# Queries and keys of a neighbourhood attention stored as 128 whole rows, with bias tables and modulation stepped at other rates

## The chip, the cores and the metric

The kernel runs on one core of a Trainium2 chip. The metric is device time of one execution in microseconds, median over several runs. The engines are named as in the profile: PE (matmuls), PEld (weight loads of PE), DVE, ACT and POOL (elementwise work), SP (issues DMAs only). ACT and POOL issue DMAs too; a DMA stands in the instruction order of the engine that issues it.

## The reference

Two blocks stand one behind the other: a two-layer block (below) and a one-layer block with dilated attention. The change is in the first one, in both of its layers. A layer projects 2048 latent and 256 context tokens (1024 wide) with one matrix and splits the result; three mixers work on the parts, among them the neighbourhood attention:

```python
hx = rmsnorm(x, norm_w[l]) * (1.0 + scale_x[:, None, :]) + shift_x[:, None, :]
(fx, fgx, nqx, nkx, nvx, ngx, gqx, gkx, gvx, ggx, zfx, zbx) = jnp.split(hx @ w_in[l], IN_SPLITS, axis=-1)
...
na_x = neighbourhood_attention(split_heads(nqx, NA_HEADS), split_heads(nkx, NA_HEADS),
                               split_heads(nvx, NA_HEADS), nkc_h, nvc_h, rpb[l])
...
# inside: 6 heads of 64, an 8 x 16 neighbourhood on a grid 64 wide, a bias from rpb, and all context keys
s_loc = jnp.einsum('brqhd,brikhd->bhrqik', qg, kg).astype(jnp.float32) + bias[None]
s_ctx = jnp.einsum('brqhd,bchd->bhrqc', qg, kc).astype(jnp.float32)
p = jax.nn.softmax(jnp.concatenate([s_loc, s_ctx], axis=-1), axis=-1)
...
x_new = x + gate_x[:, None, :] * (mix_x @ w_out[l])
```

`shift`, `scale` and `gate` (the modulation) are products of a small vector with w_ada.

## The kernel before

All matmuls on large matrices are done on a split of both operands into a hi and a lo part: three products (`MM3`) stand for one.

**The input projection** (`b1_inproj`, class `InProj`) runs once per layer as 13 blocks of output columns. `InProj.block` goes through the groups of a block (tokens); each group is 24 matmuls (8 pieces of the inner dimension, 3 products) into one PSUM tile `mm` (a pool of 5), which an `evac` function empties. Block 4 is the Fourier input (18 groups of 128 tokens in layer 0, 16 in layer 1), blocks 5 to 7 are the keys (`nk`, 128 columns each), 8 to 10 the queries (`nq`), 11 and 12 gates (`fg`). Blocks 5 to 12 have groups of 512 tokens: four and one of 256 in layer 0; in layer 1 the queries and gates have only the four.

While a block runs, the weights of the next are made: `prep` loads 6 and then 2 pieces into one buffer `wraw` (SP, line 244), ACT writes `whi` (line 252), POOL writes `wlo` (line 253).

**Evacuation of queries and keys** (`qk_evac`): ACT writes the scaled hi part (`evh`, lines 465 and 468), DVE the lo part (`evl`, lines 466 and 469), both into tiles of one pool of four (`ev`). POOL then stores them to DRAM (line 455, names `kl`, `ql`): hi and lo for keys, hi, lo and hi again for queries. The scratch is `[6 heads, 3 or 2 copies, 64, TT]`, so that a store of 128 partitions is written as 2 heads of 64 rows. The two `fg` blocks store `ev` tiles to `gT` from POOL too (line 446), as 128 rows of one step.

**Extra work** is a generator, `ip.extra`, advanced `ip.rate` times after each group: `tables` makes the attention's bias tables for both layers (`Bias.make`, 17 steps a layer: POOL loads `rpt`, stores `rp`, loads 12 pieces `bt` (line 1070), DVE works on `bt` (lines 1075, 1079 and 1080), POOL stores `be` and `bi` (line 1083)); `ada` makes a part of the modulation (`Ada.part`: loads of `adaw`, 512 KB each, into two buffers on SP (line 105), 8 steps of matmuls `adaps` (line 120), a row and its store). `more` says which generator runs in blocks 4 to 6 (first) and in blocks 7 to 12 (second), each of the two with its own SBUF pool `ipa`, which takes the same memory one after the other. What is left of a generator at the end of its blocks runs there.

**The attention** (`na`) loads per group of 512 queries two tiles `Q` (hi over lo, and lo over hi; `load_q`, line 1102), and per head a tile `Ks` of keys (hi over lo; `load_k`, line 1108), one group ahead. The first of them go through POOL, all later ones through SP. Three pairs of heads times five groups are 15 query groups in layer 0, and 12 in layer 1. The attention runs beside the linear attention and other work (the mixers).

The tile framework decides the order of instructions on each engine from the order of the code and from its own estimates, and sets the waits: for operands, for the release of a buffer or of memory that a later pool takes over, and for one of eight DMA semaphores used in turn by each issuing queue.

Of the kernel before, what the change touches and what calls it, by code (L numbers as in the profile page):

```python
# [23 lines left out]
TT = T + TC  # L24
# [3 lines left out]
def f(ap):  # L28
    return ap.bitcast(F32)


def dap(ap, off, dims):
    return bass.AP(tensor=ap.tensor, offset=ap.offset + off, ap=[list(d) for d in dims])
# [34 lines left out]
def dtile(K, shape, name):  # L68
    return K.dram.tile(list(shape), F32, name=name)
# [95 lines left out]
class InProj:  # L165
# [4 lines left out]
    def __init__(s, K, w, tiles, CMAX, wp, xp, ev):  # L170
        s.K, s.w, s.tiles, s.CMAX, s.wp, s.xp, s.ev = K, w, tiles, CMAX, wp, xp, ev
        s.xt = {}
        s.late = []
        s.extra = None
        s.rate = 1
        s.hd = None
        s.XB = 3

# [95 lines left out]
    def block(s, b):  # L274
        nc = s.K.nc
        kind, segs, groups, evac, prod = s.blocks[b]
        if prod:
            s.scale(0)
            s.scale(1)
            s.produce(0)  # L280
            s.scale(2)
            s.produce(1)
        C = sum(n for _, n in segs)
        todo = b + 1 < len(s.blocks)
        s.W[b + 1] = []
        ng = len(groups)
        w = s.W[b]
        for i, g in enumerate(groups):
            if prod:
                s.produce(i + 2)  # L290
                s.scale(i + 3)
            ps = s.mm.tile([128, 512], F32, name="mm", tag="mm")

            order = [(k, x, y) for k in range(8) for x, y in MM3]
            if prod:
                order.sort(key=lambda o: (o[1], o[0]))
            for n, (k, x, y) in enumerate(order):
                st, sp = n == 0, n == 23
                if kind == "t":
                    nc.tensor.matmul(ps[:, :C], s.hT[x][:, k, 128 * g:128 * g + 128], w[k][y][:, :C], start=st, stop=sp)  # L300
                else:
                    t0, tn = g
                    nc.tensor.matmul(ps[:C, :tn], w[k][y][:, :C], s.hT[x][:, k, t0:t0 + tn], start=st, stop=sp)  # L303
            new = evac(ps, g, i) or iter(())
            next(new, None)
            s.step()
            s.late.append(new)
            if s.extra is not None:
                for _ in range(s.rate):
                    next(s.extra, None)  # L310
            want = (8 * (i + 1) + ng - 1) // ng
            while todo and len(s.W[b + 1]) < want:
                s.W[b + 1] += s.prep(s.blocks[b + 1][1], len(s.W[b + 1]))
        del s.W[b]
# [10 lines left out]
def b1_inproj(K, A, l, xsrc, mod, S, keep, more=None):  # L325


    nc, tc = K.nc, K.tc
# [3 lines left out]
    full = l == 0  # L332
# [6 lines left out]
    with ExitStack() as es:  # L339
# [108 lines left out]

        def qk_evac(nm, r0, scale):


            ns = 3 if nm == "q" else 2

            def out(x, y, t0, tn):
                nc.gpsimd.dma_start(dap(S[nm], ((r0 // 64) * ns + x) * 64 * TT + t0, [[64 * ns * TT, 2], [TT, 64], [1, tn]]), f(y[:, :tn]))

            def go(ps, g, i):
                t0, tn = g
                hi = ev.tile([128, 512], F32R, name="evh", tag="ev")
                lo = ev.tile([128, 512], F32R, name="evl", tag="ev")  # L460
                if nm == "q" and tn == 512:
                    for h in range(2):
                        src = dap_sb(ps, 32 * h + 479, [[-64, 8], [-1, 32]])
                        oh, ol = (x[:, 256 * h:256 * h + 256].rearrange("p (a b) -> p a b", b=32) for x in (hi, lo))
                        nc.scalar.activation(out=oh, in_=src, func=AF.Copy, scale=scale)
                        nc.vector.scalar_tensor_tensor(out=ol, in0=src, scalar=scale, in1=f(oh), op0=ALU.mult, op1=ALU.subtract)
                else:
                    nc.scalar.activation(out=hi[:, :tn], in_=ps[:, :tn], func=AF.Copy, scale=scale)
                    nc.vector.scalar_tensor_tensor(out=lo[:, :tn], in0=ps[:, :tn], scalar=scale, in1=f(hi[:, :tn]), op0=ALU.mult, op1=ALU.subtract)
                for x, y in ((0, hi), (1, lo), (2, hi))[:ns]:  # L470
                    out(x, y, t0, tn)
            return go

        tx = list(range(16))
# [47 lines left out]
            ip.end()  # L522
        for bs, fill in ((range(4, 7), 0), (range(7, run), 1)):
            with tc.tile_pool(name="ipa", bufs=1, side="right", reuse_waits="tile") as p:
                ip.rate = 1
                ip.raw = lambda: p.tile([128, 768], F32, name="wraw", tag="wraw", bufs=1)
                if more[fill] is not None:
                    ip.extra = more[fill](p, lambda: mm.tile([128, 512], F32, name="adaps", tag="mm"), lambda: pt.tile([128, 256], F32, name="adat", tag="pt"))
                for b in bs:
                    ip.block(b)  # L530
                for _ in ip.extra or ():
                    pass
                ip.end()
# [57 lines left out]
def b1_scratch(K, l):  # L591
    s = {}
    n = f"l{l}"
    s["vh"] = dtile(K, [2, 32, 40, 384], "vh" + n)
    s["vc"] = dtile(K, [256, 384], "vc" + n)
    s["f"] = dtile(K, [TT, 256], "f" + n)
    s["g"] = dtile(K, [TT, 768], "g" + n)
    s["gq"], s["gk"], s["gv"] = (s["g"][:, a:b] for a, b in ((0, 192), (192, 384), (384, 768)))
    s["la"] = dtile(K, [2, TT, 192], "la" + n)
    s["gT"] = dtile(K, [1024, TT], "gT" + n)  # L600
    s["h"] = dtile(K, [18 if l == 0 else 16, 128, 1024], "h" + n)
    s["q"] = dtile(K, [6, 3, 64, TT], "q" + n)
    s["k"] = dtile(K, [6, 2, 64, TT], "k" + n)
    s["mixT"] = dtile(K, [1024, TT], "mixT" + n)
    return s

# [480 lines left out]
def na(K, A, l, S, B, p, pp, nps):  # L1087

    nc = K.nc
    full = l == 0  # L1090
    groups = [(pr, g) for pr in range(3) for g in range(5 if full else 4)]

    q0 = [nc.gpsimd]
    rd = dtile(K, [3, 5, 1024], f"rd{l}")

    def load_q(pr, g):

        n = 512 if g < 4 else TC
        out = []
        for x in range(2):  # L1100
            q = p.tile([128, 2, 512], F32R, name="Q", tag="Q", bufs=4)
            q0[0].dma_start(f(q[:, :, :n]), dap(S["q"], (2 * pr * 3 + x) * 64 * TT + 512 * g, [[TT, 128], [192 * TT, 2], [1, n]]))
            out.append(q)
        return out

    def load_k(pr, hh):
        k = p.tile([128, TT], F32R, name="Ks", tag="Ks", bufs=3)
        q0[0].dma_start(f(k[:]), dap(S["k"], (2 * pr + hh) * 128 * TT, [[TT, 128], [1, TT]]))
        return k

    def load_vc(pr):
# [1166 lines left out]
def program(nc, tc, A, out):  # L2278
    K = Ctx()
    with ExitStack() as es:  # L2280
# [21 lines left out]
                    yield from part  # L2302
            return go

        more = ((tables, ada((0, 2))), (None, ada((1, 2))))

        S = [b1_scratch(K, l) for l in range(2)]
        S2 = b2_scratch(K)
        keeps = [ExitStack() for l in range(2)]
# [69 lines left out]
```

## Time and profile before

| | |
|---|---|
| median of 3 runs | 4462.8 us (4462.49 to 4475.38) |
| profiled execution | 4484.28 us, its span 4482.5 us |
| PE busy | 4165.0 us (93%) |
| DVE, ACT, POOL busy | 1757.1, 1646.8, 1526.9 us (39, 37, 34%) |
| mean granted clock of PE | 0.949 |
| DMA | 637.13 MB, 610668 packets, mean 142 GB/s |

The granted clock is a share of TensorE's full speed; 1.0 and 0.5 are its two levels. The profile is of one execution that took 21.5 us more than the median of the runs. PE is the engine that is nearest to always busy, so what counts is where it stands idle and where its clock is granted at half.

### The profile page before, as it was taken

The page shows a single profiled execution, that of the slowest core. Times are in us where ns is not written, and L with a number is a line of the kernel's source. Part 1 is how long each engine was busy: PE and PEld are TensorE (multiplying, and loading weights), DVE is VectorE, ACT ScalarE, POOL GpSimd, SP SyncE. Part 2 cuts the span into 40 slices and gives each one's busy share as a digit, 9 for nine tenths or more (in the row PEclk, how much of TensorE's full clock was granted, in tenths as well). Part 3 has the DMA queues.
Part 4 walks back from the last instruction along what each step waited for, and adds up shares of the span by engine and source line. Part 5 has one row for each costly group of instructions (what it writes and reads, how often), then busy time and mean ns, then how long its engine had stood idle before and what let it go on. Part 6 is the DMA issues. An engine that isn't in the chain of part 4 may idle for free.

```text
span 4482.5 us, 79595 instructions
## 1 busy us (share of the span) xinstructions
PE 4165.0 (93%) x29633; PEld 3517.6 (78%) x29633; DVE 1757.1 (39%) x4996; ACT 1646.8 (37%) x4121; POOL 1526.9 (34%) x1944
## 2 busy tenths in 40 slices
PE   7999679989999999987898998999999999998998
PEld 6988469867767799865896777889998877776886
DVE  5331003366752362200235674553640025665222
ACT  5141114355661151511435656242222215664221
POOL 4234333212422332233321241444742340553333
PEclk8999889999999999998998999999999998888999
DMA  6435435466566544245546666542331156745221
GB/s 201 144 106 123 120 96 192 152 179 184 180 214 203 170 139 144 87 100 112 189 159 179 179 194 193 176 142 81 103 109 50 62 172 158 173 127 147 91 94 61
DMA packets 610668, 637.13 MB, mean 142 GB/s; under 512 B 188632, under 2 KB 487964, under 8 KB 606826
## 3 DMA queue, kind: packets, MB, share of 16 engines
q1 hardware_dynamic: 499546, 477.70, 36.3%
q0 software_dynamic: 99184, 136.27, 10.6%
q10 hardware_dynamic: 11552, 18.08, 1.1%
q8 instruction: 235, 3.85, 0.4%
q14 instruction: 151, 1.24, 0.1%
HBM read 424.26 MB, written 207.09 MB: 141 GB/s over the span
## 4 chain that ended last, share of the span: by engine, by line
PE 38%; issue 4%; DMA 3%; POOL 3%; DVE 2%; ACT 1%; SPq 1%; POOLq 0%; DVEq 0%; ACTq 0%
PE mm L300 7%; PE mm L303 5%; PE ops L1420 4%; PE tps L2173 3%; PE tps L2232 3%; PE gps L580 2%; PE apo L1827 2%; PE apt L1807 2%; PE aps L1786 2%; PE aps L1789 2%; POOL wlo L253 1%; PE po L1224 1%; PE go L991 1%; PE pl L1199 1%; PE gc L918 1%
## 5 line engine op out<-in xcount | busy, mean ns | idle before, releaser
L300 PE MATMUL mm<-whi,hTh 128*128 128x304 f32 (+2 forms) x1424 | 422.0, 300 | 2.1 <-ACT hTh L220 2.1
L300 PE MATMUL mm<-wlo,hTh 128*128 128x304 f32 (+2 forms) x1424 | 419.7, 298 | 0.0
L253 POOL TENSOR_TENSOR wlo<-wraw,whi 128x128 fp32r<-128x128 f32 (+3 forms) x384 | 224.1, 612 | 485.7 <-ACT whi L252 475.9
L300 PE MATMUL mm<-whi,hTl 128*128 128x304 f32 (+2 forms) x1424 | 380.9, 296 | 0.0
L303 PE MATMUL mm<-hTh,whi 128*128 128x512 f32 x600 | 239.9, 400 | 64.7 <-ACT whi L252 30.5
L300 PE MATMUL mm<-whi,h2h 128*128 128x256 f32 x1024 | 293.0, 290 | 2.4 <-ACT h2h L220 2.4
L300 PE MATMUL mm<-wlo,h2h 128*128 128x256 f32 x1024 | 285.7, 283 | 0.0
L300 PEld LDWEIGHTS mm<-whi,hTh 128*128 128x128 f32 x1424 | 270.6, 190 | 2.9 <-ACT hTh L220 2.8
L300 PE MATMUL mm<-whi,h2l 128*128 128x256 f32 x1024 | 272.1, 284 | 0.0
L300 PEld LDWEIGHTS mm<-wlo,hTh 128*128 128x128 f32 x1424 | 270.5, 190 | 0.0
L300 PEld LDWEIGHTS mm<-whi,hTl 128*128 128x128 f32 x1424 | 256.9, 189 | 1.1 <-issue 1.1
L252 ACT ACTIVATE whi<-wraw 128x128 fp32r<-128x128 f32 (+3 forms) x416 | 122.9, 356 | 339.5 <-DMA wraw<-in_w_in 322.2
L303 PE MATMUL mm<-hTh,wlo 128*128 128x512 f32 x600 | 236.6, 394 | 8.4 <-POOL wlo L253 8.4
L580 PE MATMUL gps<-gh,whi 128*128 128x256 f32 x816 | 233.8, 287 | 6.2 <-ACT gh L155 6.2
L303 PE MATMUL mm<-hTl,whi 128*128 128x512 f32 x600 | 234.7, 391 | 0.0
L580 PE MATMUL gps<-gh,wlo 128*128 128x256 f32 x816 | 232.9, 286 | 0.0
L580 PE MATMUL gps<-gl,whi 128*128 128x256 f32 x816 | 232.3, 285 | 0.0
L1420 PE MATMUL ops<-owh,omh 128*128 128x512 f32 x544 | 214.0, 393 | 0.0
L1420 PE MATMUL ops<-owh,om 128*128 128x512 f32 x544 | 211.9, 390 | 0.1
L1420 PE MATMUL ops<-owl,omh 128*128 128x512 f32 x544 | 211.7, 389 | 0.0
L303 PEld LDWEIGHTS mm<-hTh,whi 128*128 128x128 f32 x600 | 119.4, 199 | 99.8 <-ACT whi L252 31.2
L300 PEld LDWEIGHTS mm<-whi,h2h 128*128 128x128 f32 x1024 | 194.8, 190 | 2.7 <-ACT h2h L220 2.7
(482 smaller groups left out, 11041.1 us busy)
## 6 DMA issues: line engine op xcount, KB each, us to landing
qkv<-gl SPq DMA_DIRECT2D x72, 384.0 KB
adaw<-in_w_ada SPq DMA_DIRECT2D x48, 512.0 KB
Q<-ql SPq DMA_DIRECT2D x44, 512.0 KB
hl<-evk SPq DMA_DIRECT2D x68, 256.0 KB
gl<-hl SPq DMA_DIRECT2D x17, 1024.0 KB
om<-mixTl SPq DMA_DIRECT2D x34, 512.0 KB
gTl<-ev POOLq DMA_DIRECT2D x67, 256.0 KB, 3.9
wraw<-in_w_in SPq DMA_DIRECT2D x32, 512.0 KB
```

The lines of the kernel that those rows point to most:

```text
L252: nc.scalar.activation(out=hi[:, :C], in_=raw[:, k], func=AF.Copy)
L253: (eng or nc.gpsimd).tensor_tensor(out=lo[:, :C], in0=raw[:, k], in1=f(hi[:, :C]), op=ALU.subtract)
L300: nc.tensor.matmul(ps[:, :C], s.hT[x][:, k, 128 * g:128 * g + 128], w[k][y][:, :C], start=st, stop=sp)
L303: nc.tensor.matmul(ps[:C, :tn], w[k][y][:, :C], s.hT[x][:, k, t0:t0 + tn], start=st, stop=sp)
L580: nc.tensor.matmul(ps.rearrange("p (t n) -> p t n", t=2), W[b][k][y][:, 128 * j:128 * j + 128], h[x][:, :, k], start=n == 0, stop=n == 23)
L1420: nc.tensor.matmul(ps, m[x][:, k], W[k][y][:, 512 * n:512 * n + 512], start=k == j == 0, stop=k == 7 and j == 2)
L1786: nc.tensor.matmul(ps[:, hh, cs], q[:, qs], k[:, ks], start=True, stop=False, skip_group_check=True)
L1789: nc.tensor.matmul(ps[:, hh, cs], q[h, qs], kl[h, ks], start=False, stop=True, skip_group_check=True)
L1807: nc.tensor.transpose(pt[:, hh, c], ec[:, hh, 128 * c:128 * c + 128], K.ident)
L1827: nc.tensor.matmul(o[rr], V[:, r * (16 // DIL[br]) + b - full + c * full, rr], et[:, hh, c], start=not full or c == 0, stop=not full or c ...
L2173: nc.tensor.matmul(ps, m[u][:, k], b.Wo[k][v][:, 512 * n:512 * n + 512], start=k == b.KS[0] and j == 0, stop=k == b.KS[7] and j == 2)
L2232: nc.tensor.matmul(ps, X[x][:, k], b.Wg[k][y][:, ns], start=j == 0, stop=j == 23)
```

## The change

Stores: the scratch of queries and of keys becomes `[3 pairs of heads, 2, 128, TT]`, a store's destination 128 rows of one step, and the third store of the queries (hi again) goes. Loads: each `Q` and each `Ks` is loaded by two DMAs of 64 partitions. Extra work: in layer 0 the tables take 2 steps a group, `ada` 1 step every second group; in layer 1 `ada` moves from blocks 7 to 12 into blocks 4 to 6, also 1 step every second group.

```diff
--- before.py
+++ after.py
@@ -173,6 +173,7 @@
         s.late = []
         s.extra = None
         s.rate = 1
+        s.due = 0
         s.hd = None
         s.XB = 3
 
@@ -306,7 +307,9 @@
             s.step()
             s.late.append(new)
             if s.extra is not None:
-                for _ in range(s.rate):
+                s.due += s.rate
+                while s.due >= 1:
+                    s.due -= 1
                     next(s.extra, None)
             want = (8 * (i + 1) + ng - 1) // ng
             while todo and len(s.W[b + 1]) < want:
@@ -448,12 +451,6 @@
 
         def qk_evac(nm, r0, scale):
 
-
-            ns = 3 if nm == "q" else 2
-
-            def out(x, y, t0, tn):
-                nc.gpsimd.dma_start(dap(S[nm], ((r0 // 64) * ns + x) * 64 * TT + t0, [[64 * ns * TT, 2], [TT, 64], [1, tn]]), f(y[:, :tn]))
-
             def go(ps, g, i):
                 t0, tn = g
                 hi = ev.tile([128, 512], F32R, name="evh", tag="ev")
@@ -467,8 +464,8 @@
                 else:
                     nc.scalar.activation(out=hi[:, :tn], in_=ps[:, :tn], func=AF.Copy, scale=scale)
                     nc.vector.scalar_tensor_tensor(out=lo[:, :tn], in0=ps[:, :tn], scalar=scale, in1=f(hi[:, :tn]), op0=ALU.mult, op1=ALU.subtract)
-                for x, y in ((0, hi), (1, lo), (2, hi))[:ns]:
-                    out(x, y, t0, tn)
+                for x, y in enumerate((hi, lo)):
+                    nc.gpsimd.dma_start(S[nm][r0 // 128, x, :, t0:t0 + tn], f(y[:, :tn]))
             return go
 
         tx = list(range(16))
@@ -522,7 +519,8 @@
             ip.end()
         for bs, fill in ((range(4, 7), 0), (range(7, run), 1)):
             with tc.tile_pool(name="ipa", bufs=1, side="right", reuse_waits="tile") as p:
-                ip.rate = 1
+
+                ip.rate = 2 if full and not fill else 0.5
                 ip.raw = lambda: p.tile([128, 768], F32, name="wraw", tag="wraw", bufs=1)
                 if more[fill] is not None:
                     ip.extra = more[fill](p, lambda: mm.tile([128, 512], F32, name="adaps", tag="mm"), lambda: pt.tile([128, 256], F32, name="adat", tag="pt"))
@@ -599,8 +597,9 @@
     s["la"] = dtile(K, [2, TT, 192], "la" + n)
     s["gT"] = dtile(K, [1024, TT], "gT" + n)
     s["h"] = dtile(K, [18 if l == 0 else 16, 128, 1024], "h" + n)
-    s["q"] = dtile(K, [6, 3, 64, TT], "q" + n)
-    s["k"] = dtile(K, [6, 2, 64, TT], "k" + n)
+
+    s["q"] = dtile(K, [3, 2, 128, TT], "q" + n)
+    s["k"] = dtile(K, [3, 2, 128, TT], "k" + n)
     s["mixT"] = dtile(K, [1024, TT], "mixT" + n)
     return s
 
@@ -1099,13 +1098,15 @@
         out = []
         for x in range(2):
             q = p.tile([128, 2, 512], F32R, name="Q", tag="Q", bufs=4)
-            q0[0].dma_start(f(q[:, :, :n]), dap(S["q"], (2 * pr * 3 + x) * 64 * TT + 512 * g, [[TT, 128], [192 * TT, 2], [1, n]]))
+            for y in range(2):
+                q0[0].dma_start(f(q[64 * y:64 * y + 64, :, :n]), S["q"][pr, x ^ y].rearrange("(h r) t -> r h t", h=2)[:, :, 512 * g:512 * g + n])
             out.append(q)
         return out
 
     def load_k(pr, hh):
         k = p.tile([128, TT], F32R, name="Ks", tag="Ks", bufs=3)
-        q0[0].dma_start(f(k[:]), dap(S["k"], (2 * pr + hh) * 128 * TT, [[TT, 128], [1, TT]]))
+        for x in range(2):
+            q0[0].dma_start(f(k[64 * x:64 * x + 64]), S["k"][pr, x, 64 * hh:64 * hh + 64])
         return k
 
     def load_vc(pr):
@@ -2302,7 +2303,7 @@
                     yield from part
             return go
 
-        more = ((tables, ada((0, 2))), (None, ada((1, 2))))
+        more = ((tables, ada((0, 2))), (ada((1, 2)), None))
 
         S = [b1_scratch(K, l) for l in range(2)]
         S2 = b2_scratch(K)
```

In POOL's queue in layer 0, at the first key block (`kl` are stores of keys; `bt`, `be`, `bi` belong to the bias tables; `wlo` are weights of a later block), stood before:

```order
L1083 DMA bi_82<-bt 32x2x1200 x3
L455 DMA kl_93<-evh 2x64x512
L455 DMA kl_93<-evl 2x64x512
L455 DMA kl_93<-evh 2x64x512
L455 DMA kl_93<-evl 2x64x512
L1070 DMA bt<-rp_4320 32x15x40 x2
L455 DMA kl_93<-evh 2x64x512
L455 DMA kl_93<-evl 2x64x512
L1070 DMA bt<-rp_4320 32x15x40 x2
L455 DMA kl_93<-evh 2x64x512
L455 DMA kl_93<-evl 2x64x512
L1070 DMA bt<-rp_4320 32x15x40 x2
```

and now stands:

```order
L1082 DMA bi_82<-bt 32x2x1200 x3
L468 DMA kl_93<-evh 128x512
L468 DMA kl_93<-evl 128x512
L468 DMA kl_93<-evh 128x512
L1069 DMA bt<-rp_4058 32x15x40 x12
L468 DMA kl_93<-evl 128x512
L468 DMA kl_93<-evh 128x512
L468 DMA kl_93<-evl 128x512
L468 DMA kl_93<-evh 128x512
L254 TENSOR_TENSOR wlo<-wraw,whi 128x128 x2
L1082 DMA be_83<-bt 32x2x1200 x3
L468 DMA kl_93<-evl 128x512
```

The twelve loads of the second table's `bt`, two behind each pair of stores before, now stand in one row behind the third store, and the stores of `be` follow within the same block.

In SP's queue in layer 0, from the weights of block 7 on (`wraw` are weights of the projection in pieces of 6 and 2, `adaw` weights of the modulation, `adagb` its bias), stood before:

```order
L244 DMA wraw<-in_w_in 128x6x128
L244 DMA wraw<-in_w_in 128x2x128
L105 DMA adaw<-in_w_ada 128x1024 x2
L244 DMA wraw<-in_w_in 128x6x128
L144 DMA adagb<-in_b_ada 2x256 x4
L244 DMA wraw<-in_w_in 128x2x128
L244 DMA wraw<-in_w_in 128x6x128
L105 DMA adaw<-in_w_ada 128x1024
L244 DMA wraw<-in_w_in 128x2x128
L105 DMA adaw<-in_w_ada 128x1024
L244 DMA wraw<-in_w_in 128x6x128
L105 DMA adaw<-in_w_ada 128x1024 x3
```

and now stands:

```order
L245 DMA wraw<-in_w_in 128x6x128
L245 DMA wraw<-in_w_in 128x2x128
L245 DMA wraw<-in_w_in 128x6x128
L105 DMA adaw<-in_w_ada 128x1024 x2
L144 DMA adagb<-in_b_ada 2x256 x4
L245 DMA wraw<-in_w_in 128x2x128
L245 DMA wraw<-in_w_in 128x6x128
L245 DMA wraw<-in_w_in 128x2x128
L245 DMA wraw<-in_w_in 128x6x128
L245 DMA wraw<-in_w_in 128x2x128
L245 DMA wraw<-in_w_in 128x6x128
L105 DMA adaw<-in_w_ada 128x1024 x2
```

The pair of `adaw` loads stands behind the six-piece load of the next block's weights instead of ahead of it, and the later `adaw` loads stand further back, with whole blocks of weights between them.

In POOL's queue in layer 0, where the attention starts (`ke`, `ss` and `oacc` belong to the linear attention), stood before:

```order
L1108 DMA Ks<-kl_93 128x2304
L1102 DMA Q<-ql_92 128x2x512 x2
L1108 DMA Ks<-kl_93 128x2304
L935 TENSOR_TENSOR ke<-qkv,e_8366 128x192
L1141 DMA vl<-vhl_85 110x4x128
L59 TENSOR_SCALAR ss<-ss 128x4
L1126 DMA bias<-bi_82 32x880
L60 TENSOR_TENSOR ss<-ss,mhalf 128x4
```

and now stands:

```order
L1109 DMA Ks<-kl_93 64x2304 x2
L934 TENSOR_TENSOR ke<-qkv,e_8351 128x192
L1102 DMA Q<-ql_92 64x2x512 x3
L59 TENSOR_SCALAR ss<-ss 128x4
L1102 DMA Q<-ql_92 64x2x512
L934 TENSOR_TENSOR ke<-qkv,e_8456 128x192
L60 TENSOR_TENSOR ss<-ss,mhalf 128x4
L1109 DMA Ks<-kl_93 64x2304
L1015 TENSOR_TENSOR oacc<-oacc,ss 128x384
L59 TENSOR_SCALAR ss<-ss 128x4
L1109 DMA Ks<-kl_93 64x2304
```

The three loads that the first scores need (keys of one head, two `Q` tiles) have become six, and the last of them and the second head's keys stand behind more of the linear attention's work.

## Rows read from the trace of the kernel before

**Rows 1.** Busy time by stretch: us, PE, PEld, DVE, ACT, POOL, clock, DMA share, GB/s
```profile
397.17:422.40 25.23, 25.23 (x122) 20.77 (x121) 2.50 (x4) 3.97 (x11) 15.36 (x25) 1.00 0.45 109
371.98:669.68 297.70, 224.23 (x1026) 178.19 (x1024) 26.88 (x52) 37.35 (x111) 107.55 (x169) 0.87 0.46 110
1898.07:1920.42 22.35, 22.35 (x98) 18.01 (x97) 2.50 (x4) 2.31 (x5) 6.46 (x10) 1.00 0.33 77
1898.07:2151.17 253.10, 205.46 (x906) 160.48 (x904) 20.88 (x43) 34.75 (x106) 85.38 (x136) 0.90 0.45 105
```

**Rows 2.** The same of line 120's matmuls alone, first stretch
```profile
371.90:669.70 297.80, 6.00 (x64) 1.35 (x64) 0.87 0.46 110
```

**Rows 3.** Waits of PE, 372 to 670: total, times, longest (us)
```profile
PE mm L303 <- ACT whi L252: 24.1, 1, 24.1
PE adaps L120 <- DMA adaw<-in_w_ada: 20.0, 3, 13.8
PE mm L303 <- DVE evl L469: 8.5, 1, 8.5
PE mm L303 <- POOL wlo L253: 8.4, 1, 8.4
PE mm L303 <- DVE evl L466: 6.9, 3, 6.0
PE mm L303 <- ACT ev L445: 5.6, 1, 5.6
```

**Rows 4.** Waits of PE, 1898 to 2151
```profile
PE adaps L120 <- DMA adaw<-in_w_ada: 28.0, 2, 15.1
PE mm L303 <- DVE evl L469: 7.0, 2, 6.3
PE mm L303 <- ACT whi L252: 6.4, 1, 6.4
PE mm L303 <- DVE evl L466: 6.2, 1, 6.2
```

**Rows 5.** DMA issues, 372 to 670: count, KB each, median us to landing
```profile
ql<-evh POOLq DMA_DIRECT2D x24, 256.0 KB, 13.6
...
kl<-evh POOLq DMA_DIRECT2D x12, 256.0 KB, 11.0
...
bt<-rp POOLq DMA_DIRECT2D x12, 75.0 KB, 11.4
```

**Rows 6.** DMA issues, 340 to 352, the first bias table
```profile
bt<-rp POOLq DMA_DIRECT2D x12, 75.0 KB, 3.4
```

**Rows 7.** The first two key stores, 378 to 380, by tile
```profile
DMA to landing us min/median/max: 9.3/10.2/11.0
```

**Rows 8.** The gate stores, 640 to 669, by tile
```profile
DMA to landing us min/median/max: 2.3/3.9/4.5
```

**Rows 9.** Waits of ACT, 372 to 670
```profile
ACT evh L468 <- DMA kl<-evh: 50.4, 10, 8.6
```

**Rows 10.** Timeline of SP, 430 to 500: start, duration, line
```profile
435.78 31.96 SPq L105 DMA_DIRECT2D adaw<-in_w_ada  x2
467.79 2.80 SPq L244 DMA_DIRECT2D wraw<-in_w_in  x1
```

**Rows 11.** Waits of SP, 372 to 670
```profile
SPq L105 <- DMA bi<-bt: 15.4, 1, 15.4
```

**Rows 12.** Timeline of POOL, 300 to 386
```profile
342.13 7.89 POOL L1070 DMA_DIRECT2D bt<-rp  x12
```

**Rows 13.** Busy time in the two mixer stretches, columns as in Rows 1
```profile
760.00:1560.00 800.00, 758.11 (x6708) 606.17 (x6707) 389.98 (x1206) 358.77 (x875) 231.17 (x267) 0.98 0.60 184
2260.00:2950.00 690.00, 647.92 (x5830) 522.23 (x5829) 390.25 (x1126) 340.95 (x813) 208.73 (x257) 0.96 0.60 181
```

**Rows 14.** Waits of PE, 2260 to 2950
```profile
PE sc L1158 <- DMA Q<-ql: 1.5, 1, 1.5
```

**Rows 15.** Timeline of SP, 950 to 975
```profile
956.22 0.38 SPq L1102 DMA_DIRECT2D Q<-ql  x1
```

## The prediction

> **What bounds the kernel now.** I read the busy times first: PE is at 93%, so the question is where it stands still or is granted half its clock. The windows view then gives the two stretches in which the changed stores run, the projection blocks 5 to 12 of each layer [rows 1]. An undisturbed block of five groups takes 25.23 us, one of four 22.35 us, both at clock 1.00, with PE busy all the time. Layer 0 has eight blocks of five, 201.8 us, and 6.0 us of modulation matmuls [rows 2]: 207.8 us of work. The stretch takes 297.7 us, with PE busy for 224.2 and clock 0.87. Layer 1 has three blocks of five and five of four, 187.4 us, with the 6.0 us 193.4; its stretch takes 253.1 us, at 0.90. The surplus is 89.9 + 59.7 = 149.6 us. Of it PE is idle for 73.5 + 47.6 = 121.1 us; the other 28.5 us are work that ran longer, at a mean clock of 0.87 and 0.90 instead of 1.00.
>
> The waits of PE name what ended each idle time, and their sums are the same 73.5 and 47.6 us [rows 3, 4]. They fall into three classes:
> - **Evacuation.** DVE's evl, ACT's ev and, in layer 0, POOL's wlo: 8.5 + 6.9 + 5.6 + 8.4 = 29.4 us; in layer 1 evl and whi: 7.0 + 6.2 + 6.4 = 19.6 us. Behind all stands the landing of the stores: an ev buffer comes free when its store has landed, 11.0 us (keys) or 13.6 us (queries) after POOL issued it [rows 5], and ACT waited 50.4 us for key stores to land [rows 9]. What stands behind a waiting evacuation on ACT (whi) or behind a waiting store on POOL (wlo) is late with it.
> - **SP held by the tables.** 24.1 us, once, in layer 0. SP stood for 31.96 us at two adaw loads and only then issued the next wraw load, at 467.79 [rows 10]; the last thing waited for was bi<-bt [rows 11], since the second pool's adaw takes over the memory of the tables.
> - **Modulation.** adaps waited for adaw: 20.0 + 28.0 us.
>
> **The change part by part.**
>
> Store shape. The gate stores of the same size, already written as 128 rows of one step, land after 2.3 to 4.5 us, median 3.9 [rows 8]. The first two key stores, which follow no other key store, needed 9.3 and 11.0 us [rows 7]. So it is not the pile of stores alone, and I take 3.9 us for all new stores; the bounds are 2.3 and 11.0. What it is worth: two evacuations fit into the four ev buffers, and PE makes a group in 25.23 / 4.5 = 5.6 us (the last is a half one), so a pair may be held for 11.2 us before PE is paced by it. At 11.0 to 13.6 us plus making and issuing it is over that; at 3.9 us it is far under it, and five PSUM tiles (28 us of PE) cover a late one. The evacuation class goes, 49.0 us. The third query store goes as well; it occupied only POOL and the queue, so it counts nothing by itself once the others land fast.
>
> [...]
>
> Tables at two steps a group. The work is the same; the second table's twelve bt loads stand in a row on POOL, which took 7.89 us for the first table [rows 12]. Behind them wait a key store and later wlo. The cover is the 28 us of PSUM; without it the cost would be about 8 us. Those loads landed in 3.4 us without key stores around them and in 11.4 us among them [rows 5, 6], so bi lands earlier, within blocks 5 and 6, and SP's wraw load for block 8 stands ahead of adaw anyway. The 24.1 us go; should the tables still be late, they hold adaw, which is first needed some groups later.
>
> Modulation at one step in two groups. Steps lie 11.2 us apart instead of 5.6, with the same two buffers, so each load has twice the time; in layer 1 it starts in block 4. adaw and wraw still share SP's queue in order, and an adaw that waits for its buffer holds back the wraw behind it. Between nothing left and all 48.0 us left with their share of slow clock, 48.0 / 121.1 x 28.5 = 11.3, so 0 to 59 us, I take 15, nearer to the lower end, since the slow stores that held ACT's whi, POOL's wlo and with them SP's wraw are gone.
>
> Slow clock. Undisturbed blocks stand at 1.00 and the stretches with stops at 0.87 and 0.90 [rows 1], so I let the 28.5 us go with the stops; what stays is in the 15.
>
> Loads in halves. 27 query groups times two tiles and 12 heads are 66 loads, of which SP issues 58; so there are 58 more on SP, 0.38 us each [rows 15], 22 us, and 8 on POOL at some 0.66 (7.89 / 12), 5 us. They lie in stretches in which PE is idle for 41.9 of 800 and 42.1 of 690 us [rows 13]. PE waited 1.5 us for a Q in one of them [rows 14], as a group is loaded one group ahead. The cover is that lead; the worst is 27 us. The scheduler also orders the mixers anew, which could gain or lose: below nothing I allow 10 us, a quarter of one stretch's idle time. I take +4 us, nearest to the row, for the later first scores.
>
> [...]
>
> **The sum.** 149.6 - 15 - 4 = 130.6 us less. The profiled execution took 4484.3 us and would take 4353.7. It lies 21.5 us above the median of the runs; I put that down to this execution and take the same difference from the median: 4462.8 - 130.6 = 4332.2 us.
>
> **The rivals.**
> - **SP's queue takes over** (the weights wait in place of the evacuation). For it: wraw is one buffer, adaw still stands between its loads, with three adaw in one row at the end. Against it: within an undisturbed block the weights came in time. Price: the modulation waits stay, 48.0, and whi's 6.4, with their clock share, 12.8: 67.2 in place of the 15. Gain 149.6 - 67.2 - 4 = 78.4, 4384 us.
> - **The stores stay slow** (their landing is traffic, not shape). For it: bt loads too went from 3.4 to 11.4 us in that company, and the gate stores were measured in a later part of the stretch. Against it: the first key stores. Then evacuation stays, 49.0 with 11.5 of clock: gain 130.6 - 60.5 = 70.1, 4393 us.
> - **The halves come late** (slower). Place: the first score of each of the 27 query groups, behind four Q loads on SP instead of two, among the linear attention's loads. It decides from 130.6 / 27 = 4.8 us a group on; at 6 us, 162 us are lost and the time is 4494 us. For it: SP issues in order. Against it: [rows 14].
> [...]
> - **More goes**: nothing of the modulation waits stays and the mixers fall better by 10 us: gain 159.6, 4303 us.
>
> **How the numbers follow.** Forecast 0.64, SP's queue 0.15, slow stores 0.08, more 0.06, halves late 0.04, no gain 0.03. Differences under 0.3% (13 us) can't be told from none here. Faster are the first four, 0.93; same 0.03; slower 0.04. The forecast's own range is 4311 (whole surplus) to 4370. To leave out no more than two in ten, with the upper bounds above, the range is 4303 to 4393.
>
> **What would show it.** Right: kl and ql stores landing in about 4 us; the two stretches near 215 and 200 us with clock over 0.95; no wait of PE on evl; no SP wait at L105 of tens of us. SP's queue: PE waits on whi or adaw remain at 30 us or more. Slow stores: landings at 9 us or more. Halves: waits of PE on Q of several us, and mixer stretches longer than 800 and 690 us. The forecast is wrong if the stretches keep more than 60 us of their surplus, or if the mixers lose more than 30 us.

## The result, and the profile after

The changed kernel takes 4392.9 us (median of 4 runs, 4380.2 to 4396.3), the kernel before 4466.6 us (4 runs beside it): a ratio of 0.983, 95% interval 0.980 to 0.985. It is 73.7 us faster; the forecast was 130.6. The profiled execution after took 4396.3 us, 87.9 less than that of before. It lies 3.5 us above its median, that of before 17.7 above its own; so the comparison of the two traces is some 14 us too kind.

The windows view of the changed kernel (length; busy time and instructions of PE, PEld, DVE, ACT, POOL; granted clock; DMA share; GB/s), first the two projection stretches, then the mixers of each layer, from the first `gc` of the linear attention to the first `ops` of the output projection:

```profile
369.24:576.92 207.68, 207.68 (x1026) 167.62 (x1024) 27.98 (x52) 40.04 (x111) 80.11 (x154) 1.00 0.44 139
1843.79:2035.10 191.31, 191.31 (x884) 153.07 (x880) 20.11 (x40) 38.51 (x104) 62.77 (x123) 1.00 0.34 115
761.20:1303.80 542.60, 478.54 (x4978) 368.34 (x4978) 302.98 (x1074) 301.63 (x778) 138.34 (x186) 0.91 0.65 172
2199.00:2709.00 510.00, 459.10 (x4729) 354.46 (x4729) 282.96 (x1007) 284.72 (x721) 125.25 (x169) 0.91 0.66 177
```

The same two mixer stretches in the kernel before:

```profile
853.90:1357.00 503.10, 462.14 (x4978) 355.03 (x4978) 296.32 (x1074) 300.33 (x778) 134.46 (x182) 0.97 0.63 186
2316.40:2800.10 483.70, 443.00 (x4729) 343.25 (x4729) 281.72 (x1007) 284.43 (x721) 122.96 (x165) 0.94 0.63 186
```

Read beside [rows 1]: the projection takes 207.7 us instead of 297.7, with PE busy from the first to the last at clock 1.00, and 191.3 instead of 253.1. Of the surplus of 149.6 us nothing is left. The mixers lost: 542.6 us instead of 503.1, and 510.0 instead of 483.7, at clock 0.91 instead of 0.97 and 0.94. The sum is -90.0 - 61.8 + 39.5 + 26.3 = -86.0; all the rest of the program adds -1.9. On the page PE is now busy for 95% of the span instead of 93, which looks like a gain everywhere; the clocks say that part of it is work at half clock: by the clock records of the two traces the granted clock stood at 0.5 for 95.6 us of the mixers' 542.6 and 88.8 of the 510.0, before for 30.7 of 503.1 and 54.6 of 483.7.

The stores in layer 0's stretch of the changed kernel (name, queue, count, KB each, median us to landing), beside [rows 5]:

```profile
kl<-evh POOLq DMA_DIRECT2D x12, 256.0 KB, 2.8
kl<-evl POOLq DMA_DIRECT2D x12, 256.0 KB, 3.8
...
ql<-evh POOLq DMA_DIRECT2D x12, 256.0 KB, 2.6
ql<-evl POOLq DMA_DIRECT2D x12, 256.0 KB, 3.0
...
bt<-rp POOLq DMA_DIRECT2D x12, 75.0 KB, 2.7
```

These stores of 256 KB land in 2.6 to 3.0 us (queries) instead of 13.6 and in 2.8 to 3.8 (keys) instead of 11.0, and the tables' `bt` among them in 2.7 instead of 11.4. PE's waits of [rows 3] are gone altogether. SP's longest wait at an `adaw` is now for the buffer, behind the matmuls that use it, which costs PE nothing [rows 10, 11] (engine, line, what it waited for: sum, times, longest):

```profile
SPq L105 <- PE adaps L120: 42.7, 6, 11.5
```

In the mixers PE's waits are spread over the serial steps of the linear attention (`ga`, `gT`, `gpt`, `gu`); the keys and queries themselves are a small part. After, layer 0:

```profile
PE ga L959 <- ACT kT L950: 10.9, 13, 2.2
...
PE gT L945 <- DVE qd L939: 7.1, 8, 1.7
PE sc L1158 <- DMA Ks<-kl: 4.2, 1, 4.2
```

Before, the same stretch:

```profile
PE ga L960 <- ACT kT L951: 7.5, 9, 2.2
...
PE gT L946 <- DVE qd L940: 3.8, 4, 1.2
```

So the question is why the linear attention stands alone more often when only the attention's loads were changed.

### The profile page after: what moved, and what is told of

The parts are those of the page before. It is cut to its first block, busy times and chain, and to the rows that moved or that the text cites. A ratio compares the mean times of both kernels' runs of the same rounds, so it can differ in the third digit from the quotient of the medians.

```text
span 4394.5 us, 79619 instructions
## 1 busy us (share of the span) xinstructions
PE 4163.2 (95%) x29633; PEld 3519.0 (80%) x29633; DVE 1759.8 (40%) x4996; ACT 1657.8 (38%) x4121; POOL 1483.9 (34%) x1925
## 5 line engine op out<-in xcount | busy, mean ns | idle before, releaser
L304 PE MATMUL mm<-hTh,whi 128*128 128x512 f32 x600 | 227.9, 381 | 0.0
L304 PE MATMUL mm<-hTh,wlo 128*128 128x512 f32 x600 | 227.0, 378 | 0.0
L1181 ACT ACTIVATE el<-el,st 128x696 f32<-128x696 f32 (+2 forms) x204 | 168.5, 828 | 82.0 <-DVE st L1178 80.1
L1798 ACT ACTIVATE ae<-ae,ast 128x256 f32<-128x256 f32 (+1 forms) x384 | 171.7, 451 | 71.1 <-DVE ast L1796 71.1
```

Of the source, the lines that this page charges most:

```text
L1181: nc.scalar.activation(out=e[:, :n], in_=e[:, :n], func=AF.Exp, scale=-1.0, bias=m[:, hh, mi:mi + 1], accum_out=den[:, hh, dj:dj + 1])
L1798: nc.scalar.activation(out=ec[:, hh, cs], in_=ec[:, hh, cs], func=AF.Exp, scale=-1.0, bias=m, accum_out=d)
```

## Experiments

Each kernel ran beside the kernel before on the same chip. The runs fell on four chips, on which the kernel before had medians of 4466.9 to 4472.0 us; so some 5 us of a difference between two experiments can be the chip. In the text, "halves" means that each `Q` and `Ks` is loaded by two DMAs of 64 partitions, as in the changed kernel.

**Halves alone, in the kernel before.**

```diff
-            q0[0].dma_start(f(q[:, :, :n]), dap(S["q"], (2 * pr * 3 + x) * 64 * TT + 512 * g, [[TT, 128], [192 * TT, 2], [1, n]]))
+            for y in range(2):
+                q0[0].dma_start(f(q[64 * y:64 * y + 64, :, :n]), dap(S["q"], (2 * pr * 3 + x + y) * 64 * TT + 512 * g, [[TT, 64], [192 * TT, 2], [1, n]]))
```

> The kernel before, with one edit: each Q and each Ks is loaded by two DMAs of 64 partitions. Stores, scratch and pacing are those of before. In the build every matmul of the mixers then stands in the order of the changed kernel (first score behind 332 instead of 296 other matmuls in layer 0). Theory 1 (the halves alone cost the mixers their time, by what they do to the order of the work or by landing late): the two mixer stretches, from the first gc to the first ops, go from 503 and 484 us to about 543 and 510, the whole to 4466.6 + 66 = 4532 us. Theory 2 (the mixers lose because the projection ahead of them ends sooner and leaves them other transfers or another clock): 4467 us, stretches as before.

Measured: 4543.3 us, ratio 1.017 (1.013 to 1.020); mixers 541.9 and 515.8 us. Theory 1: the halves by themselves make the kernel slower, by 75 us, with a projection stretch in layer 0 as slow as before (300.0 us).

**The store's shape alone, with whole loads.** Rows of hi and lo alternate in the scratch (`[6, 64, 2, TT]` for keys), so that both a store and a load are 128 rows of one step.

```diff
-                nc.gpsimd.dma_start(dap(S[nm], ((r0 // 64) * ns + x) * 64 * TT + t0, [[64 * ns * TT, 2], [TT, 64], [1, tn]]), f(y[:, :tn]))
+                nc.gpsimd.dma_start(dap(S[nm], (x // 2 * 768 + 2 * r0 + x % 2) * TT + t0, [[2 * TT, 128], [1, tn]]), f(y[:, :tn]))
-                for x, y in ((0, hi), (1, lo), (2, hi))[:ns]:
+                for x, y in ((0, hi), (1, lo), (2, lo), (3, hi))[:ns]:
```

> The kernel before, with another layout of the scratch and nothing else: rows of hi and lo alternate, so that a store's destination is 128 rows of one step and a whole Q or Ks is still one DMA of 128 rows; queries are stored four times (hi and lo, lo and hi) instead of three. Pacing as before. The matmuls of the mixers stand in the order of before. Theory 1: stores land in 2.3 to 4.5 us, the mixers stay at 503 and 484 us. If the evacuation class alone goes, 49.0 us and 11.5 of clock, 4466.6 - 60.5 = 4406 us, with the SP wait at the tables and the adaw waits left; if the late stores also stood behind the tables and the modulation, up to 4466.6 - 149.6 = 4317 us. Theory 2: the mixers lose what they lost in the changed kernel in the measure in which the projection gains, so 4440 us or more.

Measured: 4343.5 us, ratio 0.972 (0.969 to 0.974), with the old pacing and one query store more than before. 125 us go by the shape of the stores alone, nearly the whole surplus; the mixers took 509.9 and 485.7 us. SP still stood at the tables, for 10.6, 10.9 and 7.8 us where the kernel before had 15.1, 15.4 and 15.6:

```profile
SPq L105 <- DMA bi<-bt: 10.9, 1, 10.9
SPq L105 <- DVE bt L1075: 10.6, 1, 10.6
SPq L105 <- DMA be<-bt: 7.8, 1, 7.8
```

but PE, over the same stretch, no longer noticed it. These are all its waits there, and the first is at the Fourier input behind it:

```profile
PE fps L675 <- DMA wf<-in_w_four: 3.4, 1, 3.4
PE mm L303 <- POOL wlo L253: 1.2, 1, 1.2
PE mm L303 <- ACT whi L252: 1.1, 2, 0.7
```

**Shape and pacing, with whole loads.** The kernel just above with the changed kernel's `due`, `rate` and `more`.

> The kernel of the run above (rows of hi and lo in turn, whole loads, four query stores), with the changed kernel's pacing as well: it differs from the changed kernel in the scratch's layout, a third and fourth query store, and in that no load is halved. The matmuls of the mixers stand in the order of before. Theory 1: projection stretches near 208 and 192 us as in the changed kernel, mixers 503 and 484 us as before, the whole 4392.9 - 66 = 4327 us, faster than both kernels. Theory 2: mixers 543 and 510 us as in the changed kernel, 4393 us. If the two stores more a group fill POOL (four issues of 0.55 us and a wlo in 5.6 us), the query blocks would be longer by some us each, up to 4350.

Measured: 4336.6 us, ratio 0.971 (0.969 to 0.972), faster than both kernels; mixers 504.2 and 486.9 us, as before. Theory 2, that the mixers pay for what the projection gains, is out. The pacing's 6.9 us lie within the two intervals.

**Pacing alone, in the kernel before.** Only `due`, `rate` and `more` as in the change.

> The kernel before with the changed kernel's pacing alone: in layer 0 two steps of the tables a group and half a step of the modulation, in layer 1 half a step of the modulation from block 4 on. Stores and loads as before. If pacing works by itself: the 24.1 us of SP and the 48.0 us of adaw waits go with 17 us of clock, 4466.6 - 89 = 4377 us. If the slow stores are what holds the rest back, the table's loads crowd with them and the waits move to evl and whi: 4440 to 4480 us. The mixers stay at 503 and 484 us by theory 1 and get longer by theory 2.

Measured: 4473.1 us, ratio 1.001 (0.999 to 1.003): nothing. In layer 0's stretch the waits for `adaw` are gone and `whi` is down from 24.1 us to 4.0, but PE waits for the evacuation instead, 45.3 us where [rows 3] had 15.4 for `evl`:

```profile
PE mm L304 <- DVE evl L469: 27.5, 5, 7.6
PE mm L304 <- DVE evl L472: 17.8, 6, 5.8
PE mm L304 <- ACT whi L253: 4.0, 1, 4.0
```

**Halves put back into the fast kernel.** The kernel of 4336.6 us, each load as two of 64 partitions.

> The kernel of rows of hi and lo in turn with the new pacing (4336.6 us), now with every Q and Ks loaded by two DMAs of 64 partitions. Nothing else. The matmuls of the mixers then stand in the order of the changed kernel. Halves as the whole cause: mixers 543 and 510 us, 4336.6 + 56 to 66 = 4393 to 4403 us. If the changed layout of the scratch has a part in the loss, less than half of that: under 4365 us.

Measured: 4399.1 us, ratio 0.985 (0.982 to 0.987); mixers 538.3 and 512.4 us. The halves cost 62.5 us and bring the time back to that of the changed kernel (4392.9 us, the intervals overlap); no part of its scratch in the loss shows.

Two things come with the halves: the loads are later, and the framework, which plans with its own estimates, sets the matmuls into another order. The next two runs separate them, by edges of issue order between the matmuls (`want` is the list of tile names in the other kernel's order, `q` the matmuls of each name):

```diff
+        prev = None
+        for c in o.want[o.n:o.n + n]:
+            i = q[c].pop(0)
+            if prev is not None:
+                o.tc.add_manual_dep(i, prev.name, mybir.DependencyInfo(mybir.DependencyClass.NoSync, mybir.DependencyReason.DATA), reason="order")
+            prev = i
```

**Whole loads, order of the changed kernel.**

> Whole loads, rows of hi and lo in turn, new pacing (4336.6 us), but the matmuls of linear attention and attention (12 tile names, 5769 matmuls) are held in the changed kernel's order by issue order alone, without a wait. The other engines are ordered anew by the framework. Order theory (the loss lies in where the attention's matmuls stand among those of the linear attention): mixers near 543 and 510 us, 4393 to 4403 us though no load is halved. Transfer theory (the loss lies in the halves' landing and in SP's and POOL's issues): 4337 us, mixers 504 and 487 us.

Measured: 4388.9 us, ratio 0.982 (0.979 to 0.985); mixers 531.6 and 510.9 us. The order alone costs 52 us, though every load is whole and PE waits for no `Ks` and no `Q` in either layer. Whole loads held by the same edges in their own order, which would show what the edges cost by themselves, were not run.

**Halves, order of before.**

> The other corner: loads in halves, rows of hi and lo in turn, new pacing, but the matmuls of linear attention and attention held in the order of before. Order theory: 4337 to 4345 us, mixers near 504 and 487 us though each load is halved. Transfer theory: PE waits for Q and Ks where it did not in the run of whole loads, above all at the first scores of a pair of heads; 4393 us or more, since the order now leaves the halves less time.

Measured: 4404.4 us, ratio 0.985 (0.983 to 0.988); mixers 542.0 and 519.1 us. So the transfer theory holds here: PE waits for the loads themselves. Layer 0:

```profile
PE sc L1164 <- DMA Ks<-kl: 15.0, 3, 6.1
...
PE sc L1164 <- DMA Q<-ql: 8.2, 1, 8.2
```

The wait of 8.2 us and one of 4.3 stand at the first scores, the other two (6.1 and 4.6 us) at the two changes of pair.

Either by itself costs about what both cost together (52 and 68 us beside 62.5). The halves do come late (this run); the framework's order for them lets the attention stand back and the linear attention run alone meanwhile, which costs as much (the run before). Neither theory was right alone. That the losses don't add up I read so: at each place PE stops either for a load or for the chain of the work put in front of it, not for both. Only PE's order was held; the other engines were ordered anew in both runs.

**Old scratch, each store as two of 64 rows.**

```diff
+                for z in range(2):
+                    nc.gpsimd.dma_start(dap(S[nm], ((r0 // 64 + z) * ns + x) * 64 * TT + t0, [[TT, 64], [1, tn]]), f(y[64 * z:64 * z + 64, :tn]))
```

> The kernel before with its own scratch, its whole loads and its pacing; only each key and query store of 128 partitions is issued as two of 64, each with a destination of 64 rows of one step: the same rows to the same places, twice the DMAs (six instead of three for a group of queries). Mixers in the order of before. If the two steps of the destination made the stores slow: they land in 2.3 to 4.5 us and the time is that of the run with rows of hi and lo in turn, 4343 us, or up to 20 us more where POOL's six issues (0.55 to 0.8 us each) and a wlo do not fit into a group's 5.6 us. If the number of rows or stores counts and not their shape, landings stay at 9 us or more and the time at 4440 us or more.

Measured: 4337.1 us, ratio 0.970 (0.968 to 0.973). The same rows go to the same places by twice as many DMAs, and land over four times as fast, layer 0's stretch:

```profile
ql<-evh POOLq DMA_DIRECT2D x48, 128.0 KB, 2.9
...
kl<-evh POOLq DMA_DIRECT2D x24, 128.0 KB, 2.7
```

The queue of POOL needed 8832 packets for 23.63 MB there; the kernel before 37872 for 23.89 MB (the DMA queue rows: packets, MB, share of 16 engines). That of the run with half stores:

```profile
q0 software_dynamic: 8832, 23.63, 37.8%
```

and that of the kernel before:

```profile
q0 software_dynamic: 37872, 23.89, 35.9%
```

The extra packets carry next to nothing: before, 32040 of the 37872 were of 4 to 16 B, 0.28 MB together (sizes of that queue's packets in the trace). In the whole stretch 32448 packets were under 512 B before and 3398 with half stores, a difference as large as that of the two rows. The data of POOL's queue went in the same pieces, 4864 packets of 4096 B in either kernel, with a median of 0.159 and 0.164 us. But of its packets of 1000 B and more, 5.9 were under way at a time before and 10.9 with half stores (means over the time with any under way, worked out from the packets' starts and lengths in the two traces).

It is the shape: one destination of two steps made the stores slow, not their number (here doubled) or size (256 KB with one step landed in 2.4 to 3.4 us in the kernel with rows in turn).

**Which halves cost?** Three kernels with the fast scratch and the new pacing: the first four loads of a layer in halves (POOL's), all later ones (SP's), and of the later ones only the keys. The condition stands in the load:

```diff
+        for y in range(2) if q0[0] is nc.sync else (None,):
+            r, m = (slice(0, 128), 128) if y is None else (slice(64 * y, 64 * y + 64), 64)
+            q0[0].dma_start(f(k[r]), dap(S["k"], ((2 * pr + hh) * 128 + 64 * (y or 0)) * TT, [[TT, m], [1, TT]]))
```

> Rows of hi and lo in turn, new pacing, whole loads (4336.6 us), but the first four loads of each layer's attention (two Ks and two Q, those that POOL issues) in halves: 8 DMAs more in the kernel instead of 66. The first score stands where it stands in the changed kernel (behind 332 instead of 296 matmuls). Theory 'the start decides' (the attention begins some 13 us later, and the first steps of the linear attention run without it): most of the 62 us is lost, 4375 to 4400 us, mixers 530 and 505 us. Theory 'each group pays' (27 query groups each a little late): 8/66 of 62 us, 4344 us, mixers 508 and 490 us.

Measured: 4334.2 us, ratio 0.969 (0.967 to 0.971): mixers 495.9 and 491.1 us: nothing lost, although the first score starts 52.3 us after the first `gc` instead of 46.4. That the start decides was wrong.

> The counterpart: the first four loads of each layer's attention whole, all later ones (issued by SP) in halves, 58 DMAs more. The first score stands where it stands in the kernel before. Theory 'the start decides': 4337 to 4350 us, mixers near 504 and 487 us. Theory 'each group pays': 58/66 of 62 us, 4391 us, mixers 535 and 509 us.

Measured: 4406.3 us, ratio 0.985 (0.983 to 0.987); mixers 539.9 and 514.9 us. The later 58 carry all of it.

> As the run with all of SP's later loads in halves (4406.3 us), but of them only the keys: four Ks a layer, 8 DMAs more instead of 58; every Q is whole. In that run the linear attention ran alone for 24 us (994 to 1018 us) around the first change of pair, where a new Ks and a new Q come together. Theory 'change of pair' (the last Ks of a pair, which waits for its buffer and is needed at once, decides): most of the loss stays, 4385 to 4406 us. Theory 'queries' (four Q loads a group instead of two fill SP's queue and its eight semaphores, and the order follows): 4334 to 4350 us, mixers near 504 and 487 us.

Measured: 4365.5 us, ratio 0.976 (0.973 to 0.979); mixers 518.2 and 500.3 us. Both theories have a part: 8 more key loads cost 29 us over the kernel of whole loads, and 50 more query loads on top of them another 41 (23 and 40 by the ratios to the kernel before beside each). Query halves alone were not run.

Where the time goes, the scores show. Each query group's first score, counted from the layer's first `gc`, can be set against the same score in the kernel of whole loads (starts of `sc` in the traces). With all later loads in halves it lags, in layer 0, by 0.1 to 8.7 us in the first pair of heads, by 5.1, 22.1, 22.7, 21.9 and 33.3 us in the five groups of the second, and by 32.8 to 38.5 us in the third. With keys alone in halves the lag is -1.1 to -0.2 us in the first pair, then -0.3, 14.8, 14.8, 11.8 and 11.0, and 12.4 to 18.0 in the third. Whole loads in the order of the changed kernel jump at the same two places, from -2.3 to 11.4 and from 11.6 to 18.3 us. So the loss does not come group by group: the greatest single part comes behind the first group of the second pair, the next towards that pair's end.

That place is a change of pair. By the code the second head's `Ks` of the new pair is loaded only when the pair's first group begins (`if g == 0 and pr: kv[pr][0].append(load_k(pr, 1))`), into one of three buffers, and is needed at once; so not every `Ks` is loaded one group ahead. SP around it with whole loads (start, length, queue, line, operation, names, count):

```profile
983.55 0.43 SPq L1111 DMA_DIRECT2D Ks<-kl  x1
990.31 1.11 SPq L1253 DMA_DIRECT2D rb<-rd  x2
991.52 1.04 SPq L1105 DMA_DIRECT2D Q<-ql  x2
```

and with the later loads in halves:

```profile
984.37 2.00 SPq L1133 DMA_DIRECT2D bias<-bi  x4
986.48 0.36 SPq L871 DMA_DIRECT2D qkv<-gl  x1
986.88 1.40 SPq L873 DMA_DIRECT2D la<-lal  x1
990.57 1.11 SPq L1257 DMA_DIRECT2D rb<-rd  x2
991.72 0.58 SPq L1260 DMA_DIRECT2D ngt<-gTl  x1
992.35 1.08 SPq L1115 DMA_DIRECT2D Ks<-kl  x2
993.53 2.91 SPq L1107 DMA_DIRECT2D Q<-ql  x4
```

The keys come at 992.4 instead of 983.6: `rb`, which waits for the store of what it loads (SP stands 2.3 us ahead of it here), stood behind them and now stands ahead. In the groups of PE's work from 994.5 to 1018.5 us of that kernel (line, names, shapes, count; busy us, mean ns; idle before and releasers) there is one score at the very end and nothing else of the attention:

```profile
L980 PE MATMUL gu<-qkv,ke 64*48 64x96 f32 x32 | 3.7, 368 | 3.0 <-DVE L L966 1.5 <-DVE VS L985 1.4
L994 PE MATMUL go<-VS,L 128*64 128x96 f32 x32 | 3.1, 373 | 1.7 <-DVE VS L985 1.7
L963 PE MATMUL ga<-L,kT 64*64 64x64 f32 x32 | 2.2, 318 | 2.2 <-ACT kT L954 2.2
...
L1164 PE MATMUL sc<-Ks,Q 128*128 128x256 f32 x1 | 0.6, 582 | 0.0
```

The windows view says PE was busy for 13.7 of those 24 us, at clock 0.54:

```profile
994.50:1018.50 24.00, 13.73 (x124) 9.33 (x124) 12.59 (x35) 3.76 (x15) 8.49 (x11) 0.54 0.84 205
```

With whole loads the same 24 us hold attention work between the steps (`po`, `pl`, `sc`, `sl`) and hardly a wait, with PE busy for 20.9 us at clock 0.98:

```profile
994.50:1018.50 24.00, 20.91 (x239) 15.76 (x239) 16.96 (x67) 11.85 (x34) 9.55 (x14) 0.98 0.81 219
```

```profile
L1227 PE MATMUL po<-tl,vl 110*64 110x128 f32 (+1 forms) x32 | 3.4, 279 | 0.0
L1202 PE MATMUL pl<-ident,el 128*110 128x128 f32 (+1 forms) x16 | 3.1, 276 | 0.0
L980 PE MATMUL gu<-qkv,ke 64*48 64x96 f32 x32 | 2.4, 249 | 0.0
...
L1160 PE MATMUL sc<-Ks,Q 128*128 128x256 f32 x6 | 2.2, 388 | 0.0
L1167 PE MATMUL sl<-Ks,Q 128*128 128x440 f32 (+1 forms) x5 | 2.1, 415 | 0.3 <-DVE st L1175 0.3
```

**Half stores with the new pacing.** Half stores with the changed pacing, scratch and loads of before.

> The kernel before with each key and query store of 128 partitions issued as two of 64 rows (4337.1 us with the old pacing), and the changed kernel's pacing. Scratch and whole loads as before. The old pacing left PE one wait of 8.9 us for whi in layer 0's stretch. If pacing takes that and nothing else: 4328 us, the fastest of all. If six store issues a group, with the tables at two steps a group, fill POOL: wlo late, 4337 us or more.

Measured: 4330.4 us, ratio 0.968 (0.965 to 0.970). PE's wait of 8.9 us for `whi` is gone. It beats the changed kernel by 62 us; against the other kernels with fast stores and SP's loads whole (4334 to 4344 us) the intervals overlap, so that it is the fastest is not shown.

## Why the prediction was partly right

- **Evacuation class (49.0 us): right, and larger.** The stores land in 2.6 to 3.8 us (3.9 was taken), and their shape alone was worth 125 us. What was wrong is the split into three classes: the tables' 24.1 and the modulation's 48.0 were counted as edits with causes of their own, but shape alone took them too (4343.5 us), and pacing alone took nothing (4473.1). They were the same delay, shown under the name of whatever came last; with the stores slow, removing one wait only showed the next.
- **Residual (15 taken, 0 to 59): 0 measured.** The two stretches lie 0.1 and 2.1 us under the work that was counted for them. The rival that SP's queue takes over did not come about.
- **Slow clock (28.5 us): right.** It went with the stops, to 1.00 in both stretches.
- **Loads in halves (+4, -10 to +27): the step that failed.** It was priced by the issue time on SP and by one wait of 1.5 us [rows 14], with "that lead" of one group as the cover. Measured: 65.8 us in the two mixer stretches, and 62.5 us when nothing but the halves was added. Three things were missed. Four issues of halves take SP 2.91 us where two of wholes take 1.04 (the rows at the change of pair), not four times 0.38. The lead of one group does not hold at a change of pair, where one `Ks` is loaded only as the pair begins: with the order of before PE's longest wait for keys, 6.1 us, stood there, and with the later loads in halves the lag grew there by 17.0 us in layer 0. And the framework reorders everything beside the loads once they are planned later; the prediction allowed 10 us of gain for that, from idle time, and for a loss no more than the 27 us of issue time, but the price includes PE's work at half clock: of layer 0's 39.5 us, busy time rose by 16.4 (the same 4978 instructions of PE, at a mean clock of 0.91 instead of 0.97) and idle time by 23.1 us.
- **The slower rival (halves late, 4494 us)** named the right edit, but not how it costs: it put the loss at the first score of each of the 27 query groups, 6 us each. The mean is 2.3 us (62.5 / 27), under its turning point of 4.8, and the scores show the loss in a few places and not in each group. Its sign, waits of PE for the loads, stayed small: 4.2 us for `Ks` and 2.3 for `Q` in layer 0, where 39.5 were lost, and none in layer 1. For the half stores, hidden behind four buffers, no cost shows: 4337.1 us, beside 4343.5 with stores of 128 rows of one step.
- **The forecast's own test** ("wrong ... if the mixers lose more than 30 us") is met, with 65.8. That the total fell into the range is luck: 4392.9 us lies at its upper end, 4393, which stood for slow stores, and these did not come. The balance behind it was wrong by +61.8 in one term and by -17.2 in another (-2.2 instead of +15). The forecast's own lower end, 4311, is 4313 by its sum (4462.8 - 149.6).
- **The baseline.** Of the 56.9 us that are missing, 42.7 are these terms (61.8 - 17.2 - 1.9); the other 14.2 are the profiled executions, 17.7 us above the median before and 3.5 after, where the same difference was carried over.

What stays open: how much of the queries' 41 us is SP's longer issue, how much later landing and how much the plan; landings of SP's loads are not in the trace. The order runs held PE alone, and what holding an order costs by itself was not measured. Neither was the tables' new rate apart from the modulation's.

## What to carry to other kernels

Give a store to DRAM a destination of one step over all its partitions, or split it where the step changes; here that was worth 125 to 130 us, whichever way it was done. When one slow resource stands behind several waits, do not price the waits as separate classes: remove it alone first, and see what is left. And where a framework plans the order from its estimates, twice the loads on a hidden path are not free (62.5 us here), even where PE hardly waits for them by name: compare the planned order of the engine that bounds the kernel, and price what moves with half clock included.

## What the runs showed of the hardware

- A store of 128 partitions whose destination has two steps (2 times 64 rows) landed in 11.0 to 13.6 us; the same rows as two stores of one step in 2.7 to 2.9 us; 128 rows of one step in 2.4 to 3.8 us (medians of layer 0, stores of 256 KB or its halves). On POOL's queue the first form took 37872 packets for 23.89 MB, the second 8832 for 23.63 MB, with 5.9 and 10.9 data packets under way at a time. Why the first form is slow no run shows.
- A half did not take half the time: the first `Ks` loads of layer 0, issued by POOL, landed after 8.5 us as halves of 576 KB and after 10.3 us as wholes of 1152 KB, the `Q` after 6.1 and 9.2 us. These are medians of two to four loads, with two halves on the way together and other traffic beside them. In the changed kernel:

```profile
Ks<-kl POOLq DMA_DIRECT2D x4, 576.0 KB, 8.5
...
Q<-ql POOLq DMA_DIRECT2D x4, 256.0 KB, 6.1
```

and in the one with whole loads:

```profile
Ks<-kl POOLq DMA_DIRECT2D x2, 1152.0 KB, 10.3
Q<-ql POOLq DMA_DIRECT2D x2, 512.0 KB, 9.2
```
